# Loading two batches of one matmul operand as single rows of 16 KB per partition, with the casts reordered to fit

## The chip, the cores and the metric

The kernel runs on one core of a Trainium2 chip. Time is device microseconds (us) of that core. Before: 124.69 us, median of 3 runs (124.65 to 124.76). Engines: PE (TensorE; PEld its weight loads), DVE (VectorE), ACT (ScalarE), SP (issues most transfers). Of the two DMA queues, q1 is fed by SP and q10 by ACT.

## The reference, cut to what matters

```python
batch, m, k, n = 16, 512, 512, 512
a: [batch, k, m] float32;  b: [batch, n, k] float32
reference = np.matmul(a.transpose(0, 2, 1), b.transpose(0, 2, 1))   # float32
```

In and out 50.33 MB: 16.78 MB each of a, b and the result.

## The kernel before

The kernel casts a (on ACT) and b (on DVE) to bf16, turns b by PE transposes, multiplies on PE, copies the result out of PSUM on DVE and ACT, and stores pairs of batches. It works in pairs: b arrives for two batches in one 2 MB load with 16 KB per partition, a as 1 MB per batch with 8 KB per partition. A partition holds KO = 4 rows of k. The order of k within a batch is free, as long as the casts of a and b agree on it.

```python
a_v = a.rearrange("b (ki ko) m -> b ki ko m", ko=KO)             # 8 KB runs
b_v = b.rearrange("(p g) (ni r) k -> p (g ni) r k", g=2, r=NR)   # 16 KB runs
LOADS = 4; PAIRS = 3; OUTS = 5        # slots for a (batches), b (pairs), results (pairs)
...
# SP, in program order, batch i
if p >= PAIRS:
    sp.wait_ge(turned, p - PAIRS + 1)
sp.dma_start(b_sb[p % PAIRS][:], b_v[p])...
if use:
    sp.wait_ge(summed, MO * (i - LOADS) + 1)     # slot of batch i-4 has been cast
if i % 2 == 0 and i // 2 >= OUTS:
    sp.wait_ge(o_out[i // 2 % OUTS], 16 * (i // 2 // OUTS))   # a store has landed
sp.dma_start(a_sb[s][:], a_v[i]).then_inc(a_in[s], 16)
...
# ACT
act.wait_ge(a_in[s], 16 * (i // LOADS + 1))
act.copy(a_bf[i % 2][:], a_sb[s][:]).then_inc(ac_go, 1)
# DVE
dve.tensor_copy(b_bf[:, r, :], b_sb[p % PAIRS][:, r, :]).then_inc(bc_go, n)
```

The stores of pairs 0 to 4 are issued by ACT, those of pairs 5 to 7 by SP, the last pair in two halves of 1 MB.

## Time and profile before

| | before | how to read it |
|---|---|---|
| time, us | 124.69 (later 124.67, n = 6) | runs lie within 0.3 us |
| span of the profiled run, us | 123.0 | time less what lies outside the program's work |
| PE / DVE / ACT busy, us | 85.2 / 56.2 / 46.8 | sums; none near the span |
| share of the 16 DMA engines, q1 + q10 | 77.3% + 20.2% | together 97.5%: the bound |
| last compute ends, us | 114.8 | 8.2 us before the end |

The lines themselves are shown in the prediction.

### The profile page before, as it was taken

How to read it: one execution, taken by the hardware profiler on the slowest of the kernel's cores; microseconds unless marked ns; L12 is line 12 of the kernel's file. 1: busy time of each engine (PE TensorE's matmuls, PEld its weight loads, DVE VectorE, ACT ScalarE, POOL GpSimd, SP SyncE). 2: the span in 40 equal slices, each digit the busy share in tenths (PEclk: the TensorE clock that was granted, in tenths of full speed). 3: DMA queues.
4: the chain of work that ended last, by engine and by line, in shares of the span. 5: the costliest groups of instructions: out<-in, count | busy, mean ns of one | idle time of the engine just before them, and what ended most of it. 6: DMA issues, size and time to landing. Idle time of an engine off the chain costs nothing. (4 is left out here: it accounts for less than half of the span.)

```text
span 123.0 us, 1080 instructions
## 1 busy us (share of the span) xinstructions
PE 85.2 (69%) x392; PEld 49.4 (40%) x400; DVE 56.2 (46%) x48; ACT 46.8 (38%) x34; POOL 0.7 (1%) x6
## 2 busy tenths in 40 slices
PE   0000949899889979979996988047999489979100
PEld 0000913474366446427544633042654354456000
DVE  0004271928648584782957430680377515513000
ACT  4050015443680962566027280029211592631200
POOL 2000000000000000000000000000000000000000
PEclk9999999999999999999999999955589999999955
DMA  3999999999999999999999999999999999999992
GB/s 69 442 426 426 410 429 440 429 410 440 426 413 440 426 413 370 450 416 434 416 426 429 445 429 424 424 426 448 421 418 426 424 426 429 426 426 426 426 429 115
DMA packets 5648, 50.33 MB, mean 409 GB/s; under 512 B 528, under 2 KB 528, under 8 KB 528
## 3 DMA queue, kind: packets, MB, share of 16 engines
q1 hardware_dynamic: 4288, 39.85, 77.3%
q10 hardware_dynamic: 1360, 10.49, 20.2%
HBM read 33.55 MB, written 16.78 MB: 409 GB/s over the span
## 5 line engine op out<-in xcount | busy, mean ns | idle before, releaser
L223 PE MATMUL o_ps<-bt_sb,a_bf 128*128 128x512 bf16 x248 | 63.6, 405 | 5.7 <-PEq L198 4.6
L223 PEld LDWEIGHTS o_ps<-bt_sb,a_bf 128*128 128x128 bf16 x256 | 28.8, 116 | 35.7 <-issue 13.8
L139 ACT CAST a_bf<-a_sb 128x2048 bf16<-128x2048 f32 x16 | 30.4, 1902 | 32.3 <-DMA a_sb<-in_a_dram 32.3
L209 PE MATMUL bt_ps<-identity,b_bf 128*128 128x128 f32 x144 | 23.7, 317 | 23.4 <-PEq L198 23.4
L148 DVE COPY o_sb<-o_ps 128x1024 f32<-128x1024 f32 x16 | 19.6, 1225 | 36.0 <-PE o_ps L223 36.0
L209 PEld LDWEIGHTS bt_ps<-identity,b_bf 128*128 128x128 f32 x144 | 21.6, 211 | 28.6 <-issue 27.6
L148 ACT COPY o_sb<-o_ps 128x1024 f32<-128x1024 f32 (+1 forms) x17 | 16.4, 963 | 34.8 <-PE o_ps L223 34.8
L156 DVE CAST b_bf<-b_sb 128x2048 bf16<-128x2048 f32 x16 | 19.4, 1219 | 17.3 <-DMA b_sb<-in_b_dram 17.3
L165 DVE COPY bt_sb<-bt_ps 128x1024 f32<-128x1024 f32 x16 | 19.5, 1216 | 3.2 <-PE bt_ps L209 3.2
L139 ACT ACT_TABLE_LOAD x1 | 1.3, 1283 | 0.9 <-PEq L269 0.9
L125 POOL TENSOR_SCALAR_AFFINE_SELECT identity<-identity 128x128 f32<-128x128 f32 x1 | 0.3, 294 | 0.2 <-POOL identity L123 0.2
L123 POOL MEMSET identity<- 128x128 f32 x1 | 0.2, 205 | 0.7 <-POOLq L51 0.7
L269 POOL MEMSET const-bfloat16-1.0<- 128x1 bf16 x1 | 0.1, 102 | 0.0
L269 POOL MEMSET const-uint8-127<- 128x1 uint8 x1 | 0.1, 102 | 0.0
L269 POOL MEMSET const-float32-0.0<- 128x1 f32 x1 | 0.1, 99 | 0.2 <-issue 0.2
L269 POOL MEMSET const-float32-1.0<- 128x1 f32 x1 | 0.1, 99 | 0.0
## 6 DMA issues: line engine op xcount, KB each, us to landing
a_sb<-in_a_dram SPq DMA_DIRECT2D x16, 1024.0 KB, 15.0
b_sb<-in_b_dram SPq DMA_DIRECT2D x8, 2048.0 KB, 16.2
out_dram<-o_sb ACTq DMA_DIRECT2D x5, 2048.0 KB, 15.9
out_dram<-o_sb SPq DMA_DIRECT2D x2, 2048.0 KB, 13.2
out_dram<-o_sb SPq DMA_DIRECT2D x2, 1024.0 KB, 8.0
```

Source lines behind the costliest of these rows:

```text
L123: pool.memset(identity[:], 0.0).then_inc(id_go, 1)
L125: pool.affine_select(out=identity[:], in_=identity[:], compare_op=mybir.AluOpType.not_equal, fill=1.0, base=0, pattern=[[-1, P]], channel_ ...
L139: act.copy(a_bf[i % 2][:], a_sb[s][:]).then_inc(ac_go, 1)
L148: copy(o_sb[i // 2 % OUTS][:, i % 2, rm, :], o_ps[h][:, p, :]).then_inc(go, 1)
L156: dve.tensor_copy(b_bf[:, r, :], b_sb[p % PAIRS][:, r, :]).then_inc(bc_go, n)
L165: dve.tensor_copy(bt_sb[g][:].rearrange("p j (ni r) -> p j ni r", r=NR), bt_ps[:].rearrange("p j r (g ni) -> p g j ni r", g=2)[:, g],).the ...
L209: last = pe.transpose(bt_ps[:, j, r, :], w[:, r, j, :], identity[:])
L223: last = pe.matmul(o_ps[h][:, q, :], a_r[:, rk, 2 * h + q, :], bt_h[:, rk // 2, rk % 2, :], start=(rk == 0), stop=(rk == KO - 1),)
L269: nc = _bacc.Bacc("TRN2", target_bir_lowering=False, num_devices=1)
```

## The change

The intent: load a the way b is loaded, with 16 KB per partition, so that fewer and larger packets carry it. For pairs 1 to 5 one load of 2 MB brings both batches: the even batch to partitions 0 to 63, the odd one to 64 to 127, each partition with 8 rows of k. The matmuls are as before (128*128 in the page) and take 4 rows in each of 128 partitions, so the cast on ACT splits in two and moves one half of the rows to the other partitions. The cast of b writes k in the matching order. The four slots of a (1 MB) become three of 2 MB.

```diff
+    a_w = a.rearrange("(p g) (ki r) m -> p (g ki) r m", g=2, r=2 * KO)
-    LOADS = 4
+    WIDE = range(1, 6)
+    LOADS = 3
-        a_sb = [sb(f"a_sb{s}", [P, KO, M], f32) for s in range(LOADS)]
+        a_sb = [sb(f"a_sb{s}", [P, 2 * KO, M], f32) for s in range(LOADS)]
...
+        def load_a(sp, i):
+            q, g = divmod(i, 2)
+            s, use = q % LOADS, q // LOADS
+            if use:
+                sp.wait_ge(summed, MO * (2 * (q - LOADS) + 1) + 1)
+            if q in WIDE:
+                sp.dma_start(a_sb[s][:], a_w[q]).then_inc(a_in[2 * s], 16)
+            else:
+                sp.dma_start(a_sb[s][:, g * KO:(g + 1) * KO], a_v[i]).then_inc(a_in[2 * s + g], 16)
...
-            act.copy(a_bf[i % 2][:], a_sb[s][:]).then_inc(ac_go, 1)
+            if q in WIDE:
+                own = slice(g * P // 2, (g + 1) * P // 2)
+                for s in range(2):
+                    copy = act.copy(to[s * P // 2:(s + 1) * P // 2], x[own, s * KO:(s + 1) * KO, :])
+            else:
+                copy = act.copy(to[:], x[:, g * KO:(g + 1) * KO, :])
+            copy.then_inc(ac_go, 1)
...
-                dve.tensor_copy(b_bf[:, r, :], b_sb[p % PAIRS][:, r, :]).then_inc(bc_go, n)
+                to, x = b_bf[:, r, :], b_sb[p % PAIRS][:, r, :]
+                if p in WIDE:
+                    to = to.rearrange("p r (s ki q) -> p r ki s q", s=2, q=KO)
+                    x = x.rearrange("p r (ki s q) -> p r ki s q", s=2, q=KO)
+                dve.tensor_copy(to, x).then_inc(bc_go, n)
```

More of the change, by code (lines that the diff above doesn't have):

```diff
@@ L65 @@
         o_ps = [ps(f"o_ps{s}", [P, MO // 2, N], f32) for s in range(2)]
-        a_in = [sem(f"a_in{s}") for s in range(LOADS)]
+        a_in = [sem(f"a_in{s}") for s in range(2 * LOADS)]
         b_in = [sem(f"b_in{s}") for s in range(PAIRS)]
@@ L89, in store, with loaded_a @@
             ).then_inc(o_out[j % OUTS] if j + OUTS < H else stored, 16)
+        def load_a(sp, i):
[7 more added lines that the diff above has]
+                sp.dma_start(a_sb[s][:, g * KO:(g + 1) * KO], a_v[i]).then_inc(a_in[2 * s + g], 16)
+        def loaded_a(q, g):
+            g = 0 if q in WIDE else g
+            uses = [u for u in range(q + 1) if u % LOADS == q % LOADS and (g == 0 or u not in WIDE)]
+            return a_in[2 * (q % LOADS) + g], 16 * len(uses)
         def run_sp(sp):
@@ L93, in run_sp @@
                 if i == 0:
-                    sp.dma_start(a_sb[0][:], a_v[0]).then_inc(a_in[0], 16)
+                    load_a(sp, 0)
                 for p in ([0] if i == 0 else [(i + 1) // 2] if i % 2 and i + 1 < B else []):
@@ L100, in run_sp @@
                     sp.dma_start(b_sb[p % PAIRS][:], b_v[p]).then_inc(b_in[p % PAIRS], 16)
-                s, use = i % LOADS, i // LOADS
-                if use:
-                    sp.wait_ge(summed, MO * (i - LOADS) + 1)
                 if i % 2 == 0 and i // 2 >= OUTS:
                     sp.wait_ge(o_out[i // 2 % OUTS], 16 * (i // 2 // OUTS))
-                if i:
-                    sp.dma_start(a_sb[s][:], a_v[i]).then_inc(a_in[s], 16)
+                if i and not (i % 2 and i // 2 in WIDE):
+                    load_a(sp, i)
             for j in range(H - TAIL, H - 1):
@@ L136, in cast_a @@
         def cast_a(act, i):
-            s = i % LOADS
-            act.wait_ge(a_in[s], 16 * (i // LOADS + 1))
-            act.copy(a_bf[i % 2][:], a_sb[s][:]).then_inc(ac_go, 1)
+            q, g = divmod(i, 2)
+            sem_, value = loaded_a(q, g)
+            x, to = a_sb[q % LOADS], a_bf[i % 2]
+            act.wait_ge(sem_, value)
+            if q in WIDE:
[5 more added lines that the diff above has]
+            copy.then_inc(ac_go, 1)
         def copy_out(eng, i, rm, go):
```

## The prediction

> **What bounds the kernel now.** I read the page's table of slices first, then the table by stage, then the waits.
>
> ```profile
> PE   0000949899889979979996988047999489979100
> DVE  0004271928648584782957430680377515513000
> ACT  4050015443680962566027280029211592631200
> DMA  3999999999999999999999999999999999999992
> q1 hardware_dynamic: 4288, 39.85, 77.3%
> q10 hardware_dynamic: 1360, 10.49, 20.2%
> ```
>
> The DMA row is full from the second slice to the last but one, while every engine has slices with little work. The two queues together take 77.3% + 20.2% = 97.5% of 16 engines' 123.0 us, that is 119.9 us. The bound is the 50.33 MB that the 16 DMA engines carry. The stages say the same:
>
> ```profile
> 2.50:20.00 17.50, 6.11 (x22) 4.15 (x23) 4.72 (x4) 3.76 (x2) 0.00 (x0) 1.00 1.00 424
> 20.00:44.00 24.00, 22.27 (x105) 12.22 (x105) 15.73 (x14) 11.29 (x9) 0.00 (x0) 1.00 1.01 427
> 44.00:62.00 18.00, 15.92 (x82) 9.71 (x84) 12.19 (x11) 9.20 (x7) 0.00 (x0) 1.00 1.00 413
> 62.00:90.00 28.00, 20.10 (x86) 11.56 (x87) 11.89 (x11) 10.59 (x8) 0.00 (x0) 0.82 1.01 430
> 90.00:114.80 24.80, 20.76 (x101) 11.75 (x102) 11.68 (x10) 10.70 (x9) 0.00 (x0) 1.00 1.01 426
> 114.80:123.00 8.20, 0.00 (x0) 0.00 (x0) 0.00 (x0) 0.01 (x1) 0.00 (x0) 0.65 0.72 306
> ```
>
> The columns are the stretch, its length, PE, PEld, DVE, ACT and POOL busy us, then clock, DMA share and GB/s. DMA share is 1.00 in every stretch but the first 2.5 us and the last 8.2 us. From 20 to 62 PE is nearly full as well (22.27 of 24.00 us): here compute paces the loads, through the buffers, without letting the DMA queues run dry. After the last compute at 114.8 us the DMA still moves 306 GB/s x 8.2 us = 2.5 MB; only 1 MB of it is the last half store. So the transfers lag behind compute by about 1.5 MB, or 1.46 MB / 425 GB/s = 3.4 us: compute could end some 3 us later and the end would hardly move.
>
> ```profile
> DVE o_sb L148 <- PE o_ps L223: 36.0, 15, 5.6
> ACT o_sb L148 <- PE o_ps L223: 34.8, 13, 4.8
> ACT a_bf L139 <- DMA a_sb<-in_a_dram: 32.3, 6, 10.3
> DVE b_bf L156 <- DMA b_sb<-in_b_dram: 17.3, 3, 10.8
> ```
>
> ACT waits 32.3 us for a to land and DVE 17.3 us for b: compute is fed by transfers. The chain of waits goes back only to 108 us and stops at ACT at 114.2 us, since behind that lies a transfer. It is of no use here.
>
> [...] an 8 KB packet takes 309 ns (median), a 16 KB packet of b 611 ns, so two 8 KB packets cost 7 ns more than one of 16 KB. [...] in 6 us stretches in which both queues have work, packet counts on the two are near equal (for example 139 on q10 against 126 on q1), although the q1 packets may be twice as long. [...] The trace has 1219 ns for the cast of b. [...]
>
> **The change part by part.**
>
> *Loads.* Ten 1 MB loads of a become five of 2 MB. 1280 packets of 8 KB become 640 of 16 KB, 40 per DMA engine. Saved: 40 x 7 ns = 0.28 us. From 20 to 44 us, with loads alone, the records have 313 and 615 ns, so 11 ns a pair there; 0.3 to 0.4 us is the most I can find. Five semaphore packets per engine of 9 ns each are saved too: 0.05 us. This lies on the path that sets the end, since the DMA engines do.
>
> *Issue.* Five fewer issues of a on SP, about 0.33 us each. SP is not on the path: it waits for buffers most of the time. Worth 0.
>
> *Cast of a on ACT.* Each of ten casts of 128 x 2048 becomes two of 64 x 2048, because the data must move between partition halves. If a copy costs by elements per partition, each still takes 1902 ns:
>
> ```profile
> L139 ACT CAST a_bf<-a_sb 128x2048 bf16<-128x2048 f32 x16 | 30.4, 1902 | 32.3 <-DMA a_sb<-in_a_dram 32.3
> L156 DVE CAST b_bf<-b_sb 128x2048 bf16<-128x2048 f32 x16 | 19.4, 1219 | 17.3 <-DMA b_sb<-in_b_dram 17.3
> ```
>
> So ACT gains 10 x 1.90 = 19.0 us, 46.8 to about 66 us. Does it fit where compute paces? In the timeline from 34 to 55 us a pair of batches takes 10.5 us (ACT copies out the even batches at 33.5, 44.0 and 54.6). ACT would need four 1.90 us casts and two 1.01 us copies: 9.6 us of 10.5. In order: the copy of the even batch at 44.04 would wait for the cast behind the copy of 40.16, which would then end at 41.1 + 3.8 = 44.9 us. PE wants that cast at about 45.9 us, so it is in time by 1 us, and the copy out slips by 0.9 us, which PE asks for only at its second half near 48.9 us. Nothing of it reaches PE. Later than 62 us ACT has 10.59 us busy in 28. So beside other work: 0.
>
> *Cast of b on DVE.* Ten of the sixteen casts become four-dimensional: read contiguously, written in runs of 4 bf16 elements. [...] In the tight stage DVE is 15.73 of 24 us busy; [...] the timeline shows gaps of 1.3 and 2.2 us ahead of its copies out. Also about 0.
>
> *Buffers.* Four slots of 1 MB become three of 2 MB: reads run up to 2 MB further ahead. A pair's load is now released by the first quarter of batch 2q-5, where batch 2q waited for batch 2q-4, so it is issued a batch earlier, and the first eight loads put 12 MB in the queue before any wait instead of 10. The smallest backlog I find before, counting bytes issued less bytes moved, is some 2 MB (5 us), near 41 and 61 us. It grows. A batch that is first of its pair lands 1 MB (2.5 us) later, as it waits for its partner: [...] ACT reaches its cast at 24.2 us. In time, narrowly.
>
> *Sum.* -0.28 - 0.05 = about -0.3 us: 124.69 - 0.3 = **124.4 us**.
>
> **The rivals.** *A: ACT becomes the pace.* For it: 9.6 of 10.5 us is close, and issuing stores (0.4 us each) and any cost of crossing partitions are not in it. Against it: even 1 us more per pair over five pairs is 5 us of lost compute progress, in a stage with loads far ahead, and after 62 us ACT idles for data long enough to take most of it back. Stores would start later; the end would move by perhaps 1 us, or if the queues run dry, 2 to 3: 125.5 to 127.5 us. *B: turns at the packet level.* While 16 KB packets of both a and b face 8 KB packets of the stores, the stores get a third of the bytes where they got a half beside a. Store 0 lands later, and the load of pair 5 waits for it on SP, as do the batches 12 and 14 for stores 1 and 2. For it: SP waited 32.0 us for stores before. Against it: whichever queue has work keeps the engines full, and loads held back by a store have that store in the queue. My hand count puts the last loads' issue near 87 us, where it was 86.4. If they came 5 us later the 3.4 us lag at the end would be used up: 126 us. *C: larger transfers raise the rate well beyond the packet cost*, by some 2% or more: 122 us. Against it: the share is 1.00 already and the packets of b, already 16 KB, are only 1.1% faster per byte.
>
> **Range and chances.** The three runs before lie within 0.11 us. The transfer bound gives 124.3 to 124.5; I allow 0.6 below for what larger transfers could save elsewhere, and 0.9 above for a part of A or B. Faster by over 2% (below 122.2) needs C: 0.01. Slower by over 2% (above 127.2) needs A or B with dry queues: 0.03. Within: 0.96.
>
> **What would show it.** The DMA row still full, the two queue shares about 97% together of a like span, packets down from 5648 by 640 of data and 80 of semaphores to 4928. The cast of a at 1.90 us with 20 instances of 64 partitions, ACT near 66 us busy. The cast of b at 1.2 us (right)[...]. The wait of ACT for a shorter, that for PE shorter. Digits under 9 in the DMA row mid-span would make the prediction wrong, as would packets of 16 KB longer than 611 ns, or a stretch after the last compute in which only the last half store is left.

640 merges at 7 ns (0.28 us over 16 engines) and 80 semaphore packets at 9 ns (0.05 us) come from the packet records and make 0.33 us, hence 124.4 us; issues, casts and buffers enter it with 0. That the cast of b stays at 1.2 us, and that a copy over 64 partitions takes as long as one over 128, was the assumption, and the run tests both. Rival B rests on packet counts of the trace alone. Besides those quoted: from 60 to 66 us 146 packets of 8 KB started on q1 beside 167 on q10 (the stores have 53% of the bytes), from 52 to 58 us 106 of 16 KB beside 103 of 8 KB (33%). For the 313 and 615 ns I find 312 and 613 over all packets of 20 to 44 us, again 11 ns a pair.

## More of the kernel before

The trace also has a record for each DMA packet, with size and time taken. They are the measure of the change, so here they are, added up over one profiled execution of each kernel (us/16 is the time of all packets divided by the 16 DMA engines):

```
records              before: count, median, us/16     changed: count, median, us/16
8 KB, q1 (a, out)    2816, 309 ns, 55.59              1536, 309 ns, 30.20
16 KB, q1 (b, a)     1024, 611 ns, 39.22              1664, 611 ns, 64.00
8 KB, q10 (out)      1280, 309 ns, 24.74              1280, 309 ns, 24.73
semaphores            528,   9 ns,  0.30               448,   9 ns,  0.25
sum                              119.84                           119.18
```

## The result, and the profile after

The changed kernel takes 124.28 us (median of 6 runs, 124.07 to 124.42) against 124.67 us (median of 6, 124.44 to 124.76). The ratio is 0.9969, with a 95% interval from 0.9956 to 0.9981. A ratio here is the mean time of one kernel's fast runs over that of the other's in the same rounds, so it is not quite the ratio of the medians quoted. Executions over 1.5% slower than the fastest of the same kernel are left out of the means. The 0.3% is small and clear of noise: the interval is a gain of 0.24 to 0.55 us.

These are, from the page of the changed kernel, the rows of the table of slices and the two queues:

```profile
PE   0000949799799979979994950593999599798000
DVE  0005272837839575692759340039295542703000
ACT  4140015684997999799797008997221864803000
DMA  3999999999999999999999999999999999999992
q1 hardware_dynamic: 3568, 39.85, 77.1%
q10 hardware_dynamic: 1360, 10.49, 20.2%
```

The DMA row is as full as before, on a span of 122.5 us. What changed in plain view is ACT: fuller by far from slice 10 to 22, and still not on the path. q1 has 720 packets fewer for the same 39.85 MB. The stages of the changed kernel, with the columns of before:

```profile
2.50:20.00 17.50, 6.23 (x23) 4.21 (x24) 4.72 (x4) 3.80 (x2) 0.00 (x0) 1.00 1.01 429
20.00:44.00 24.00, 21.61 (x107) 12.07 (x105) 16.22 (x14) 18.62 (x12) 0.00 (x0) 1.00 1.00 426
44.00:62.00 18.00, 16.55 (x86) 9.98 (x87) 10.56 (x10) 16.21 (x12) 0.00 (x0) 1.00 1.00 419
62.00:90.00 28.00, 18.47 (x88) 10.31 (x87) 13.21 (x12) 16.11 (x10) 0.00 (x0) 0.88 1.01 430
90.00:113.80 23.80, 20.46 (x101) 11.41 (x99) 11.30 (x10) 10.84 (x9) 0.00 (x0) 1.00 1.01 428
113.80:122.50 8.70, 0.00 (x0) 0.00 (x0) 0.00 (x0) 0.00 (x0) 0.00 (x0) 0.61 0.75 317
```

From 44 to 62 us ACT is busy 16.21 of 18.00 us (9.20 before) and PE still 16.55 (15.92 before). The groups of the casts, and the waits that answer to those of before:

```profile
L164 ACT CAST a_bf<-a_sb 64x2048 bf16<-64x2048 f32 x20 | 38.0, 1899 | 7.6 <-DMA a_sb<-in_a_dram 7.3
L166 ACT CAST a_bf<-a_sb 128x2048 bf16<-128x2048 f32 x6 | 11.4, 1901 | 18.4 <-DMA a_sb<-in_a_dram 18.4
L189 DVE CAST b_bf<-b_sb 128x2048 bf16<-128x2048 f32 x16 | 19.4, 1219 | 22.7 <-DMA b_sb<-in_b_dram 22.7
```

```profile
DVE o_sb L176 <- PE o_ps L256: 29.9, 14, 3.4
DVE b_bf L189 <- DMA b_sb<-in_b_dram: 22.7, 3, 10.6
ACT o_sb L176 <- PE o_ps L256: 19.6, 11, 4.7
ACT a_bf L166 <- DMA a_sb<-in_a_dram: 18.4, 5, 10.4
ACT a_bf L164 <- DMA a_sb<-in_a_dram: 7.3, 1, 7.3
```

A copy over 64 partitions takes as long as one over 128 (1899 and 1901 ns), so ACT pays twice. (Half of the twenty copies also move their rows to the other 64 partitions; all twenty lie between 1896 and 1902 ns.) ACT pays out of its waits: for PE 34.8 us before and 19.6 us now, for a 32.3 us before and 18.4 + 7.3 = 25.7 us now. The cast of b, ten of sixteen reordered, costs the same 1219 ns.

### The profile page after: what moved, and what is told of

The parts are those of the page before. It is cut to its first block, busy times and chain, and to the rows that moved or that the text cites. A ratio compares the mean times of both kernels' runs of the same rounds, so it can differ in the third digit from the quotient of the medians.

```text
span 122.5 us, 1093 instructions
## 1 busy us (share of the span) xinstructions
PE 83.3 (68%) x400; PEld 48.0 (39%) x400; DVE 56.0 (46%) x48; ACT 66.9 (55%) x44; POOL 0.7 (1%) x6
## 3 DMA queue, kind: packets, MB, share of 16 engines
q1 hardware_dynamic: 3568, 39.85, 77.1%
## 5 line engine op out<-in xcount | busy, mean ns | idle before, releaser
L256 PE MATMUL o_ps<-bt_sb,a_bf 128*128 128x512 bf16 x256 | 64.9, 402 | 8.7 <-PEq L231 8.2
L164 ACT CAST a_bf<-a_sb 64x2048 bf16<-64x2048 f32 x20 | 38.0, 1899 | 7.6 <-DMA a_sb<-in_a_dram 7.3
L242 PE MATMUL bt_ps<-identity,b_bf 128*128 128x128 f32 x144 | 22.1, 302 | 20.8 <-PEq L231 20.8
L176 DVE COPY o_sb<-o_ps 128x1024 f32<-128x1024 f32 x16 | 19.6, 1224 | 29.9 <-PE o_ps L256 29.9
L242 PEld LDWEIGHTS bt_ps<-identity,b_bf 128*128 128x128 f32 x144 | 20.5, 209 | 25.7 <-issue 24.5
L189 DVE CAST b_bf<-b_sb 128x2048 bf16<-128x2048 f32 x16 | 19.4, 1219 | 22.7 <-DMA b_sb<-in_b_dram 22.7
L176 ACT COPY o_sb<-o_ps 128x1024 f32<-128x1024 f32 (+1 forms) x17 | 16.4, 964 | 19.7 <-PE o_ps L256 19.6
L166 ACT CAST a_bf<-a_sb 128x2048 bf16<-128x2048 f32 x6 | 11.4, 1901 | 18.4 <-DMA a_sb<-in_a_dram 18.4
L198 DVE COPY bt_sb<-bt_ps 128x1024 f32<-128x1024 f32 x16 | 19.4, 1214 | 2.7 <-PE bt_ps L242 2.7
```

Source lines behind the costliest of these rows:

```text
L164: copy = act.copy(to[s * P // 2:(s + 1) * P // 2], x[own, s * KO:(s + 1) * KO, :])
L166: copy = act.copy(to[:], x[:, g * KO:(g + 1) * KO, :])
L176: copy(o_sb[i // 2 % OUTS][:, i % 2, rm, :], o_ps[h][:, p, :]).then_inc(go, 1)
L189: dve.tensor_copy(to, x).then_inc(bc_go, n)
L198: dve.tensor_copy(bt_sb[g][:].rearrange("p j (ni r) -> p j ni r", r=NR), bt_ps[:].rearrange("p j r (g ni) -> p g j ni r", g=2)[:, g],).the ...
L242: last = pe.transpose(bt_ps[:, j, r, :], w[:, r, j, :], identity[:])
```

## The experiments

Eleven kernels ran. Theory one (**packets**): the gain is the constant cost of a packet (7 ns by the records above: two of 8 KB take 2 x 309 ns, one of 16 KB 611), paid by the DMA engines, which set the end; all other parts are hidden. Rival: the gain comes from deeper buffers and earlier loads, and the packets are beside the point. A second rival: the doubled casts cost something that the packets pay back.

### Only the packets undone

```diff
-                sp.dma_start(a_sb[s][:], a_w[q]).then_inc(a_in[2 * s], 16)
+                for h in range(2):
+                    c = slice(h * KO, (h + 1) * KO)
+                    sp.dma_start(a_sb[s][:, c], a_w[q][:, c]).then_inc(a_in[2 * s], 16)
-            return a_in[2 * (q % LOADS) + g], 16 * len(uses)
+            return a_in[2 * (q % LOADS) + g], sum(32 if u in WIDE else 16 for u in uses)
```

> The changed kernel with each wide load issued as two loads of 8 KB per partition: slots, releases, casts and order stay as changed, only the packets (and five semaphore packets per DMA engine) go back. Packet theory: the 0.3 to 0.4 us gain is all packets, so it is lost: 124.6 to 124.7 us. Rival, the gain comes from deeper buffers and earlier issue: it stays at 124.3 us. If the doubled cast of a costs something that the packets pay back, this run comes out above the kernel before, at 124.8 us or more.

Measured: 124.82 us (124.64 to 125.07, n = 6), ratio to the kernel before 1.0015 (1.0001 to 1.0029). The gain is gone, with buffers, order and casts all as changed. That speaks for packets and against buffers. It speaks against the granted PE clock too: that is 0.94 to 0.95 in the changed kernel's runs and 0.92 to 0.94 in those of the kernel before, and this run has 0.935 to 0.952 with about the time of the kernel before. The time is 0.14 us above the kernel before, which is the sign that the expectation set for the second rival. It is at the edge of its interval; the run with one cast, below, looks for it.

### Only the buffers changed

```diff
-    WIDE = range(1, 6)
+    WIDE = range(0)
```

> No pair is wide: loads of 1 MB, 8 KB packets and the plain casts of before, but three slots of two batches with the changed kernel's release rule. Packet theory: as before, 124.6 to 124.7 us. Rival, deeper buffers: 124.3 us.

Measured: 124.67 us (124.36 to 124.77, n = 6), ratio 0.9993 (0.9979 to 1.0007). Three slots of two batches alone are worth nothing. The buffer rival is out.

### Smaller packets in the kernel before

```diff
-    a_v = a.rearrange("b (ki ko) m -> b ki ko m", ko=KO)
+    a_v = a.rearrange("b (s ki q) m -> b ki s (q m)", s=2, q=KO // 2)
```

(and the cast of b writes k in the order `ki s q`; both loads of a fill their slot as `p s (q m)`)

> The kernel before with a loaded in runs of 4 KB (two per partition and load, k reordered in the cast of b so that the result stays right). 2048 packets of 8 KB become 4096 of 4 KB, 128 more per DMA engine. Packet theory with the traces' constant term of about 7 ns per packet: 128 x 7 ns = 0.9 us, so about 125.5 us, and 4 KB packets of about 158 ns. Rival, the packet size does not matter and the gain was buffers: 124.7 us.

Measured: 125.58 us (125.56 to 125.72, n = 5), ratio 1.0074 (1.0061 to 1.0087): +0.90 us by the medians, as expected to a tenth. The tenth is luck: the 4 KB records have a median of 159 ns, so two cost 9 ns more than one of 8 KB and not the 7 ns assumed; 128 x 9 ns = 1.15 us, of which the time shows 0.9. The line of the page that says what was done (under 8 KB it was 528 before):

```profile
DMA packets 7696, 50.33 MB, mean 407 GB/s; under 512 B 528, under 2 KB 528, under 8 KB 4624
```

The same few ns per packet, forced the other way, move the time the other way, with the number of loads and of semaphore packets as before. This is the strongest support for theory one.

### All pairs wide

```diff
-    WIDE = range(1, 6)
+    WIDE = range(0, 8)
```

> All eight pairs wide. Packet theory: 24 more pairs of packets merged per DMA engine, 24 x 7 ns = 0.17 us, and three fewer semaphore packets, so 124.1 us if the later start (b lands 2.5 us later) and the later last batch stay hidden behind the transfers. Rival: start or tail come onto the path, the last pair lands as one and its batch 14 starts later, 125 to 127 us.

Measured: 125.00 us (124.61 to 125.96, n = 6), ratio 1.0034 (1.0005 to 1.0062). The rival of this run holds: fewer packets, and slower. The DMA row of this run dips near the end:

```profile
DMA  4999999999999999999999999999999999989974
```

Its first cast of a starts at 8.55 us (5.74 in the changed kernel) and its last compute ends at 118.57 us (113.44). The next runs part start from tail.

### One cast instead of two

```diff
-                for s in range(2):
-                    copy = act.copy(to[s * P // 2:(s + 1) * P // 2], x[own, s * KO:(s + 1) * KO, :])
+                copy = act.copy(to[:], x[:, g * KO:(g + 1) * KO, :])
```

> The changed kernel with the two 64-partition casts of each wide batch replaced by one 128-partition cast that moves nothing between partitions (wrong result on purpose: batches of a pair are mixed). ACT loses 10 x 1.90 us of work. Theory that this work is hidden: 124.3 us, as the changed kernel, ACT busy about 48 us. Rival, the doubled cast costs part of what the packets gain (the run with packets undone came out 0.14 us above the kernel before): 124.1 us.

Measured: 124.20 us (124.15 to 124.69, n = 6), ratio 0.9961 (0.9943 to 0.9978); the result is wrong, as meant. ACT falls to 47.0 us busy, 20 us less than in the changed kernel, and the time by 0.08 us of medians, inside the spread. The two ratios differ by 0.0008, that is 0.1 us, with an interval of about -0.2 to 0.4 us (an estimate from the two intervals). So the second rival is bounded, not out: this run and the one with the packets undone both hint at a cost of some 0.1 us, that one only just outside its interval and this one well within it.

### Wide pairs 1 to 6, and 1 to 7

```diff
-    WIDE = range(1, 6)
+    WIDE = range(1, 7)        # and, in the other run, range(1, 8)
```

> Pairs 1 to 6 wide. Packet theory: 8 more merges per DMA engine, 8 x 7 ns + 9 ns = 0.07 us, 124.2 us, if the later landing of batch 12 stays hidden. Rival, the tail is already at its limit: 124.4 us or more.

> Pairs 1 to 7 wide, so that against the all-wide run only the start is undone. If the tail was what cost the all-wide run (batch 14 waits for 15, and both casts of a last batch double, so that compute ends several us later): 124.6 to 125.2 us, last compute 3 us or more later than in the changed kernel. If the late start was what cost it: 124.1 us.

Measured: pairs 1 to 6 124.57 us (124.42 to 124.77, n = 6), ratio 0.9989 (0.9971 to 1.0006); pairs 1 to 7 124.33 us (124.11 to 124.97, n = 6), ratio 0.9980 (0.9958 to 1.0003). Neither beats the change, though their packets should give another 0.1 us. For pairs 1 to 6 the rival that was set holds (124.4 us or more). With pairs 1 to 7 the last compute ends at 117.12 us, 3.7 us later than in the changed kernel, and the span is still 122.3 us: the late tail was not enough to cost anything, and my expectation for a costly tail was wrong. Only the late start on top of it makes the all-wide run lose. How much lateness is free?

### The last batch delayed on purpose

The cast of the last batch is made again three or six times, the same data each time, with a drain of ACT between.

```diff
+                for n in range(4 if i == B - 1 else 1):      # 7 in the other run
+                    if n:
+                        act.drain()
                     copy = act.copy(to[:], x[:, g * KO:(g + 1) * KO, :])
```

> The changed kernel with the cast of the last batch made four times (the same data again, three repeats). In its trace that cast ends at 105.6 us and PE starts on it at 108.2 us, so three repeats of 1.9 us push the last compute some 3 us later, from 113.4 to about 116.5 us. Theory that the transfers lag behind compute by 3 to 4 us at the end: the time stays at 124.3 to 124.6 us. Rival, the end of compute sets the end: 127.3 us.

> The same with six repeats, 11.4 us: the last compute ends some 8.8 us later, near 122.2 us. Theory: the lag is used up, and the end follows the last compute by the 5.2 us that the run with pairs 1 to 7 wide shows between its last compute (117.1) and its end (122.3): a span of about 127.4, a time of about 129.2 us, that is 5 us more and not 8.8. Rival, compute sets the end: 133 us.

Measured: three repeats 125.65 and 125.82 us in the two fast runs (two more, 128.16 and 128.26, count as slow), ratio of the fast ones to the kernel before 1.0081 (1.0062 to 1.0100); six repeats 134.75 us (134.15 to 135.22, n = 4), ratio 1.0801 (1.0769 to 1.0834). Both expectations of the time missed, since the delay came out larger than planned: the last compute ended 5.5 and 14.4 us later, not 3 and 8.8. After its wait PE took 3.46 us for eight matmuls of the last batch where it had taken 1.99, and in the second run the last cast also began 3 us late. The last ACT copy of the changed kernel and of these two, from their timelines (start, length):

```profile
112.86 0.58 ACT L176 COPY o_sb<-o_ps 128x512 f32<-128x512 f32 x1 [0.32 <-PE o_ps L256]
```

```profile
118.33 0.59 ACT L179 COPY o_sb<-o_ps 128x512 f32<-128x512 f32 x1 [0.32 <-PE o_ps L259]
```

```profile
127.24 0.59 ACT L179 COPY o_sb<-o_ps 128x512 f32<-128x512 f32 x1 [0.33 <-PE o_ps L259]
```

Set against the spans, these seven profiled runs fall in line:

| run | last compute ends, us | span, us | difference |
|---|---|---|---|
| before | 114.82 | 123.0 | 8.2 |
| changed | 113.44 | 122.5 | 9.1 |
| pairs 1 to 7 wide | 117.12 | 122.3 | 5.2 |
| pairs 1 to 6 wide | 117.50 | 122.7 | 5.2 |
| all pairs wide | 118.57 | 123.5 | 4.9 |
| three repeats | 118.92 | 123.9 | 5.0 |
| six repeats | 127.83 | 132.8 | 5.0 |

In the last five rows the end follows the last compute by 4.9 to 5.2 us, whether compute ends at 117 or at 128 us: about 5.0 us for the last half store alone. The 5.2 us of the run with pairs 1 to 7 were known before the two delayed runs were made (the expectation uses them), so these two are a test of it. The changed kernel therefore has 9.1 - 5.0 = 4.1 us to spare, and the lateness beyond that is what the spans show: three repeats 5.5 - 4.1 = 1.4 us, six 14.4 - 4.1 = 10.3, all wide 5.1 - 4.1 = 1.0. The end is the later of two: the transfers, and the last compute plus 5 us. In the six profiled runs left out of the table the difference is 5.7 to 9.2 us, so there the transfers end later. One of them says it best: with only the buffers changed, compute ended at 117.2 us, 2.3 us later than in the kernel before, at a span of 122.9 us (123.0 there). The two runs with wide pairs to 6 and to 7 stand where the two meet, which would be why further merging of packets buys nothing; this is argued from one execution of each.

### ACT pushed past PE

```diff
-                for s in range(2):
+                for n, s in enumerate([0, 1, 1]):
+                    if n == 2:
+                        act.drain()
```

> The changed kernel with the second of the two casts of each wide batch made twice, so that a wide batch costs ACT three times 1.90 us: per pair 6 x 1.90 + 2 x 1.01 = 13.4 us against PE's 10.5. Theory that the change left ACT just under PE's pace: now ACT sets the pace from 23 to about 77 us, the load of pair 5 comes some us later and the end moves by 0 to 3 us, 124.3 to 127.3 us. Rival, ACT is far from any limit and idle time takes all of it: PE's period stays at 10.5 us and the time at 124.3 us.

Measured: 126.67 us (126.04 to 127.33, n = 4), ratio 1.0156 (1.0111 to 1.0201); slower clear of noise, by 2% or not stays open. Two successive batches of this run on ACT:

```profile
35.65 1.02 ACT L178 COPY o_sb<-o_ps 128x1024 f32<-128x1024 f32 x1
36.69 5.77 ACT L166 CAST a_bf<-a_sb 64x2048 bf16<-64x2048 f32 x3
42.48 1.02 ACT L178 COPY o_sb<-o_ps 128x1024 f32<-128x1024 f32 x1
43.52 5.77 ACT L166 CAST a_bf<-a_sb 64x2048 bf16<-64x2048 f32 x3
```

No wait stands behind any line, and a batch takes 42.48 - 35.65 = 6.83 us, a pair 13.7 us where it took 10.5: ACT sets the pace. The last loads of a are issued at 92 us instead of 82.7, the transfers slow down mid-span (311 GB/s in one slice; of 1.9 us more span than in the changed kernel, 1.5 us are packets that took longer and 0.4 us idle engines), and the time rises by some 2 us. So ACT's share in the change fits, but not by a wide margin: one more cast per wide batch and it is the bound.

### Four store buffers instead of five

```diff
-    OUTS = 5
+    OUTS = 4
```

> The changed kernel with four store buffers in place of five: the load of pair 4 waits for store 0, which is issued at 43.6 us, instead of being issued at 36.0 us. Theory that the order of loads behind stores is harmless in the change only because loads run far enough ahead: here the queues run dry once near 50 us, and later loads wait a store more each: 126 to 129 us, digits under 9 in the DMA row mid-span. Rival, the DMA engines stay full in any order: 124.3 us.

Measured: 132.95 and 133.00 us in the two fast runs (two more, 136.05 and 136.34, count as slow), ratio 1.0662 (1.0641 to 1.0682). Far worse than I had thought, and by the expected mechanism: pair 4's load is issued at 52.9 us instead of 36.0, and each later one waits again.

```profile
DMA  4999999999999988799999999779999899999993
```

The row falls below 9 at three places. Of the 8.6 us more span than in the changed kernel, 3.8 us are idle engines and 4.8 us packets that took longer than there (why they did stays open). So the order of loads behind stores can cost much; in the change, where the row stays full, it does not.

### How near the queues come to running dry

From the issue times and the packet records I counted the MB (2^20 bytes) issued and not yet moved:

```
at, us                     46    54    60    62    64
before   loads (q1)       3.5   2.5   0.9   4.5   4.1
         stores (q10)     2.0   0.9   2.0   1.6   1.2
changed  loads (q1)       4.5   2.1   0.5   0.0   4.0
         stores (q10)     2.0   1.1   2.2   1.9   1.1
```

From 46 to 60 us the changed kernel's loads move 3.9 MB, its stores 1.8 MB: 252 packets of 16 KB beside 227 of 8 KB, so about twice the bytes. Before, it was 3.6 to 2.0. Store 0 lands 18.8 us after its issue (16.7 before), the load of pair 5 waits for it, and at 62 us the load queue is empty. The wait of SP, from the changed kernel:

```profile
SPq L102 <- DMA out_dram<-o_sb: 15.8, 1, 15.8
```

That load is issued at 62.3 us, and its first packet starts at 65.9 us; no packet of a load starts between 61.4 and 65.9 us. The stores, 1.9 MB of them at 62 us, keep the DMA engines full alone over that time (share 0.97 from 60 to 62.3 us, 1.01 from 62.3 to 66). That is the same wait that costs 8 us with four store buffers, where the stores do not suffice.

## Why the prediction was right

**The bound and the sum.** Right. The DMA engines set the end, and of the predicted 0.3 us each term shows in the records: 640 merges at 7 ns over 16 engines are 0.28 us, 80 semaphore packets 0.05. The measured gain is 0.39 us by the medians. The packet times of the two profiled runs differ by 0.66 us; the 0.33 us beyond the sum lies in packets slower than the median (1.33 us of such excess before, 0.99 after). Executions with the same packets differ by as much: the run with only the buffers changed has the packets of the kernel before and sums to 119.54 us (119.84 there), the run with one cast has those of the changed kernel and sums to 119.65 us (119.18 there). So this part is not shown as an effect. The undone packets and the smaller packets settle that the packets are the cause. None of the named signs of being wrong came: the DMA row stays at 9, the 16 KB packets keep their median of 611 ns, and after the last compute 317 GB/s x 8.7 us = 2.8 MB are left, more than the last half store.

**Casts.** Right: 1899 ns over 64 partitions, ACT 66.9 us busy (66 predicted), the cast of b at 1219 ns, and no cost clear of noise, as the single cast shows ("0" is not shown closer than some 0.4 us). The margin was stated about right too: counted as 0.9 us of a pair's 10.5, it is in the trace one wait of ACT per pair, of 0.8 us, in the stretch where PE sets the pace, and one more cast per batch breaks it. That the cast of b would keep its speed was an assumption, and what it would have cost otherwise no run here shows; the trace has its sixteen instances between 1214 and 1228 ns (1215 to 1228 before). Batch 2 was in time narrowly, as said: in the changed kernel its data landed at 22.9 us and its cast began at 23.4, waiting for nothing; in the run with one cast it waited 0.7 us for its data.

**Buffers.** The step "The smallest backlog I find before [...] is some 2 MB [...] It grows" failed. Counted again, the smallest before is 2.5 MB, near 41 us (2.6 near 61). In the changed kernel the backlog grows early (7.8 MB at 28 us where it was 3.8), but at 62 us, where it matters, it shrinks to 1.9 MB in both queues together. I had the near equal packet counts of the two queues among the rivals (the stores' share of the bytes from 46 to 60 us fell from 36% to 31%, near the third that B names), and did not carry them into this step. That it did no harm is in part luck: the stores then in their queue sufficed to keep the engines full, and with four store buffers they did not. A slip beside it: seven loads, not eight, put the 12 MB in the queue.

**Last loads.** "My hand count puts the last loads' issue near 87 us": it was 82.7 us. Earlier than before, not later, so the later loads on which rival B hung its 126 us did not come.

**The lag at the end.** The claim of some 3 us (3.4 by bytes) held in kind. Measured against the 5.0 us of a lone last store it is 8.2 - 5.0 = 3.2 us in the kernel before and 4.1 us in the changed one.

**The rivals.** C (a much higher rate) did not come. What A and B feared does cost time when it is pushed further (126.67 us with a third cast, where ACT paces; 133.0 us with four store buffers, where loads wait behind stores), and in the change both stay below the point at which they show in the time.

## What to carry to other kernels

When the DMA row is full from end to end, as here, look first to the transfers' own cost: count packets, multiply by the difference between two packet sizes that the trace already shows, and expect about that (0.33 us forecast here, 0.39 measured). Work moved onto a waiting engine cost nothing clear of noise while its sum per period (9.6 us) stayed under the period of the engine that paces (10.5 us), and cost 2 us when it passed it (13.7 us), so compute that sum before adding it. Before stretching such a change to every batch, find what the end has to spare (here the end less last compute less the 5 us of a lone last store), since start and tail use it up.
